# Mixer groups of a hybrid decoder layer: spreading a group's state product, scan and gate over later projection tiles

## The chip, the core and the metric

The kernel runs on one core of one Trainium2 chip. The metric is the device time of one execution in microseconds; the time before is the median of 3 runs. Six engines matter: TensorE (PE in the profile, with its weight loads as PEld), VectorE (DVE), ScalarE (ACT), GpSimd (POOL), and SyncE (SP), which issues most DMAs. Each engine takes its own instructions strictly in order; semaphores order them against the others.

## What is computed

One inference step of one decoder layer, for 256 prompt tokens and 8 sample tokens (one new token for each of 8 sequences), 264 columns in all. The model's width is 2048.

```python
h += 0.5 * RMSNorm(SwiGLU_1(RMSNorm(h)))
u = RMSNorm(h)
proj = u @ w_in            # GLU a, b: 2 x 1024; z: 3072; xBC: 5120; dt: 48
...
v = silu(layernorm(causal_dwconv(glu_a * sigmoid(glu_b), w=31)))
xbc = silu(causal_dwconv(xbc, w=4))
y, h_new = ssd(x, dt, a, B, C, d_skip, h0)
yg = y * silu(z)
yg = yg * rsqrt(mean(yg * yg, per group of 384 channels) + EPS) * norm_gain
h += RMSNorm(concat(v, yg) @ w_out)
h += 0.5 * RMSNorm(SwiGLU_2(RMSNorm(h)))
h += RMSNorm(sigmoid(RMSNorm(h) @ W_gate) * (p @ W_proj))
```

The state-space part (`ssd`) has 8 groups, each with its own B and C (128 states) and 6 heads of 64 channels (384 channels, 3 tiles of 128). For the prompt it runs in two chunks of 128 tokens. For the samples it needs C times the incoming state, summed over the 128 states: y = exp(a·dt)·(C·h0) + (B·C)·x·dt + d_skip·x.

## The kernel before

All activations lie transposed: channels on the 128 partitions, the 264 tokens along the free axis. A projection's output tile is 128 channels by 264 tokens and is summed in one accumulator (`acc`, PSUM, 5 buffers). For accuracy each weight is split in two: a DMA on SP's queue brings it (`wraw`), ScalarE's cast makes the high part (`whi`, L152), VectorE subtracts it for the low part (`wlo`, L153), and each block of 128x128 takes three matmuls (L247 to L249: `whi` with both parts of the activation, then `wlo` with the first). These steps go by half-tiles of 8 blocks; an output tile of the in-projection has two half-tiles, 48 matmuls. `wraw`, `whi` and `wlo` have four buffers each, and loads are issued two units ahead.

The layer runs as a first feed-forward (to about 793 us), the mixer's in-projection (817 to 1344), its out-projection with LayerNorm and residual (to 1586), the second feed-forward (to 2318), and a per-layer embedding. The change lies in the mixer.

The in-projection has 81 output tiles in the order `IN_ORDER` (L44): dt, then for each of 8 groups B, C, three x tiles (x0, x1, x2), three z tiles (z0, z1, z2). Pairs of tiles of the GLU (gb, ga), 8 of them, stand inside the groups that `GLU_IN` (L40) lists, behind x0, and the rest at the end. After each output tile the loop at L809 emits its own work: `do_conv` (L609) for B, C and x, a short convolution of three steps on VectorE and a Silu on ScalarE; `act(..., Silu)` for z; `do_glu` for ga, whose 30 taps of the long convolution (L216, `y<-v,vec,y`) go into a list `bg`; and then up to 4 pieces of `bg` (10 in the out-projection). When the last pair is done, `do_ln`, the LayerNorm over the GLU's channels, is put at the list's end; its results are read by the last eighth-parts of the out-projection (`gemm_pair(range(CM))`).

Three functions carry a group's own work:

- `ssd` (L697), emitted after x2. Its first part is the prompt's: transposes of x and B (L707, L708), B·C (L721), the chunk states (L733), the outputs (L748). Its second part is the samples': B and C of the samples as rows (L761, L762), through DRAM to all partitions (`cbc`), then six times: load a piece of the state (`h0`, 3 buffers; the profile calls it `h<-in_hst`), multiply it with `cbc` on GpSimd (L773), reduce it on VectorE (L774, `ych<-h`). Then the sample's y.
- `gate` (L789), emitted after x0 of the next group by `finish_gate`: y times silu(z) on VectorE (`h<-h,h 128x792`), three squares on ScalarE, two additions on GpSimd (`run<-run,tmp`), their sum over partitions by a matmul with ones (L299, in `SumSq.total`), logarithm and exponential, and the scaled output.
- `decays` (L676), after x0: the decay factors of a group.

What sets the order: the program is written once for all engines, and a scheduler places each engine's instructions by its own simulated times; what was written earlier has precedence among what is ready. Small matmuls take one of three PSUM buffers (`ps`) in turn. ScalarE's function tables are loaded by `table` (L231): Silu on one side, logarithm and exponential on the other need a load at each change, and the calls are kept in program order.

## Time and profile before

| what | value |
|---|---|
| median of 3 runs | 2449.36 us (2447.6 to 2455.64) |
| the profiled execution's own time | 2442.84 us |
| its span, first to last instruction | 2441.1 us |
| mean granted TensorE clock | 0.991 |

| stage, us from the span's start | TensorE idle, us | VectorE busy | ScalarE busy |
|---|---|---|---|
| in-projection, 817 to 1344 | 20.8 | 82% | 58% |
| out-projection with residual, 1344 to 1586 | 9.1 | 77% | 54% |
| second feed-forward, 1586 to 2318 | 2.9 | 57% | 42% |

A row of a timeline reads: start, duration in us, engine, line, operation, output <- inputs, how many in a row, and in brackets how long the engine stood idle before it and what ended that. A row of the waits: what waited <- what it waited for, then total us, times, longest. A row of the windows: the stretch and its length, busy time of each engine with instructions in brackets, the granted clock, the share of the DMA engines, GB/s. A row of the groups: count | busy us in total, mean ns of one | idle time before, and what ended it. Lines are those of the kernel before.

### The profile page before, as it was taken

The page shows a single profiled execution, that of the slowest core. Times are in us where ns is not written, and L with a number is a line of the kernel's source. Part 1 is how long each engine was busy: PE and PEld are TensorE (multiplying, and loading weights), DVE is VectorE, ACT ScalarE, POOL GpSimd, SP SyncE. Part 2 cuts the span into 40 slices and gives each one's busy share as a digit, 9 for nine tenths or more (in the row PEclk, how much of TensorE's full clock was granted, in tenths as well). Part 3 has the DMA queues.
Part 4 walks back from the last instruction along what each step waited for, and adds up shares of the span by engine and source line. Part 5 has one row for each costly group of instructions (what it writes and reads, how often), then busy time and mean ns, then how long its engine had stood idle before and what let it go on. Part 6 is the DMA issues. An engine that isn't in the chain of part 4 may idle for free.

```text
span 2441.1 us, 47358 instructions
## 1 busy us (share of the span) xinstructions
PE 2365.9 (97%) x19432; PEld 2339.6 (96%) x19432; DVE 1584.4 (65%) x2273; ACT 1179.6 (48%) x1761; POOL 357.2 (15%) x353
## 2 busy tenths in 40 slices
PE   8999999999999999999999999899999999999996
PEld 8999999999999889999999999899999999999996
DVE  6554455545557858989798975866545655555585
ACT  6444444433456465565655554644444443344463
POOL 2500000000015212121212111400000000000152
PEclk9999999999999999999999999999999999999998
DMA  7655555555556666676666557467666776675653
GB/s 246 216 183 184 183 183 184 185 184 182 182 172 213 197 202 197 202 223 204 206 214 199 180 168 234 139 234 244 231 207 228 243 235 207 222 237 194 196 172 115
DMA packets 165242, 489.89 MB, mean 201 GB/s; under 512 B 25456, under 2 KB 42272, under 8 KB 165024
## 3 DMA queue, kind: packets, MB, share of 16 engines
q1 hardware_dynamic: 165024, 486.86, 61.2%
q8 instruction: 152, 2.49, 0.4%
q14 instruction: 66, 0.54, 0.1%
HBM read 465.65 MB, written 22.42 MB: 200 GB/s over the span
## 4 chain that ended last, share of the span: by engine, by line
PE 82%; DVE 7%; DMA 4%; issue 3%; ACT 3%; POOL 1%; SPq 0%; ACTq 0%; DVEq 0%; POOLq 0%
PE acc L248 27%; PE acc L247 27%; PE acc L249 27%; DVE wlo L153 2%; ACT whi L152 1%; DMA h<-in_hst 1%; POOL h L213 1%; DVE h L213 1%; DVE y L216 1%; DVE tmp L216 1%; DVE act L216 1%; DMA cbc<-d_bc 1%; DMA wraw<-in_w 1%; PE ps L299 1%; POOL run L213 0%
## 5 line engine op out<-in xcount | busy, mean ns | idle before, releaser
L249 PE MATMUL acc<-act,wlo 128*128 128x264 f32 x6320 | 1796.9, 285 | 4.5 <-DVE wlo L153 4.4
L248 PE MATMUL acc<-act,whi 128*128 128x264 f32 x6320 | 1783.5, 283 | 14.6 <-DVE act L216 7.7
L247 PE MATMUL acc<-act,whi 128*128 128x264 f32 x6320 | 1766.0, 283 | 15.9 <-ACT whi L152 8.5
L153 DVE TENSOR_TENSOR wlo<-wraw,whi 128x1024 fp32r<-128x1024 f32 (+1 forms) x806 | 993.4, 1234 | 594.5 <-ACT whi L152 588.8
L152 ACT CAST whi<-wraw 128x1024 fp32r<-128x1024 f32 (+1 forms) x806 | 828.4, 1032 | 959.6 <-PE acc L248 710.9
L247 PEld LDWEIGHTS acc<-act,whi 128*128 128x128 f32 x6320 | 1190.5, 190 | 19.1 <-ACT whi L152 8.7
L248 PEld LDWEIGHTS acc<-act,whi 128*128 128x128 f32 x6320 | 1188.4, 188 | 20.3 <-DVE act L216 10.0
L249 PEld LDWEIGHTS acc<-act,wlo 128*128 128x128 f32 x6320 | 1187.2, 188 | 8.5 <-DVE wlo L153 6.7
L213 POOL TENSOR_TENSOR run<-run,tmp 128x264 f32<-128x264 f32 x135 | 129.7, 961 | 956.8 <-ACT tmp L240 953.3
L213 POOL TENSOR_TENSOR s<-s,eap 128x1024 f32<-128x1024 f32 x24 | 48.3, 2012 | 596.8 <-DMA s<-in_hst 573.2
L216 DVE SCALAR_TENSOR_TENSOR y<-v,vec,y 128x251 f32<-128x251 f32 (+23 forms) x240 | 117.2, 508 | 1.2
L213 POOL TENSOR_TENSOR h<-h,cbc 128x512 f32<-128x512 f32 x48 | 72.1, 1521 | 165.5 <-DMA cbc<-d_bc 77.8
L216 DVE SCALAR_TENSOR_TENSOR s<-bb,xds,s 128x128 f32<-128x128 f32 x192 | 52.6, 346 | 58.7 <-POOL s L213 58.7
L213 DVE TENSOR_TENSOR tmp<-acc,rr 128x264 f32<-128x264 f32 x104 | 44.8, 431 | 59.4 <-PE acc L249 59.2
L255 ACT CAST act<-tmp 128x264 fp32r<-128x264 f32 x120 | 48.7, 410 | 60.8 <-DVE tmp L213 47.1
L213 DVE TENSOR_TENSOR tmp<-tmp,acc 128x264 f32<-128x264 f32 x88 | 37.6, 428 | 41.0 <-PE acc L249 40.1
L213 DVE TENSOR_TENSOR act<-tmp,act 128x264 fp32r<-128x264 f32 x120 | 54.2, 457 | 0.0
L240 ACT ACTIVATE tmp<-tmp 128x264 f32<-128x264 f32 x112 | 47.0, 420 | 8.1 <-DVE tmp L213 7.8
L213 DVE TENSOR_TENSOR y<-y,acc 128x264 f32<-128x264 f32 x80 | 33.9, 424 | 23.9 <-PE acc L249 23.9
L240 ACT ACTIVATE tmp<-y 128x264 f32<-128x264 f32 x67 | 28.0, 425 | 43.6 <-DVE y L213 42.5
L774 DVE TENSOR_REDUCE ych<-h 128x4 f32<-128x512 f32 x48 | 32.4, 677 | 16.3 <-POOL h L213 16.2
L216 DVE SCALAR_TENSOR_TENSOR act<-h,vec,act 128x264 fp32r<-128x264 f32 x48 | 35.2, 755 | 6.5 <-ACT act L240 6.5
(148 smaller groups left out, 793.0 us busy)
## 6 DMA issues: line engine op xcount, KB each, us to landing
wraw<-in_w SPq DMA_DIRECT2D x774, 512.0 KB, 4.5
h<-in_hst SPq DMA_DIRECT2D x48, 256.0 KB, 4.1
s<-in_hst SPq DMA_DIRECT2D x24, 512.0 KB, 6.3
out_nss<-s SPq DMA_DIRECT2D x24, 512.0 KB, 2.8
wraw<-in_w SPq DMA_DIRECT2D x32, 256.0 KB, 3.8
ab<-d_cs SPq DMA_DIRECT2D x16, 384.0 KB, 4.8
cbc<-d_bc SPq DMA_DIRECT2D x8, 512.0 KB, 4.3
bb<-d_bc SPq DMA_DIRECT2D x8, 512.0 KB, 6.0
```

The costliest lines, as they stand in the source:

```text
L152: nc.scalar.copy(hi, raw)
L153: nc.vector.tensor_tensor(out=lo, in0=raw, in1=hi.bitcast(F32), op=ALU.subtract)
L213: return (eng or nc.vector).tensor_tensor(out=out, in0=in0, in1=in1, op=op)
L216: return nc.vector.scalar_tensor_tensor(out=out, in0=in0, scalar=scalar, in1=in1, op0=op0, op1=op1)
L240: i = nc.scalar.activation(out=out, in_=in_, func=func, bias=bias, scale=scale)
L247: nc.tensor.matmul(acc, hi, x[:, 0, :], start=first, stop=False)
L248: nc.tensor.matmul(acc, hi, x[:, 1, :], start=False, stop=False)
L249: nc.tensor.matmul(acc, lo, x[:, 0, :], start=False, stop=last)
L255: nc.scalar.copy(t[:, 0, :], x)
L299: nc.tensor.matmul(p, ones, s, start=i == 0, stop=i == len(self.parts) - 1)
L774: nc.vector.tensor_reduce(out=ych[:, j, b : b + 4], in_=h0, op=ALU.add, axis=AX.X)
```

## The change

A group's work is spread over later tiles. `ssd` keeps the prompt's part and is emitted after z0 instead of x2. The sample's part becomes three functions: `sample_rows` (the rows of B and C and their trip through DRAM) after x0; `sample_state` (two state pieces: load, product) after x1, x2 and z0, whose reductions are emitted at the next call, the last at z1; `sample_out` (the rest) after z2. `gate` becomes `gate_begin` (multiplication, squares, additions), emitted after the convolution of the next group's B, and `gate_end` (the sum, logarithm, exponential, output), after that of the next C. `GLU_IN` has three groups in place of four, so three pairs stand inside groups and five at the end. Which buffers `v` takes and when the mixer's memory is closed follow the length of `GLU_IN`, as before.

```diff
--- before.py
+++ after.py
@@ -37,7 +37,7 @@
 FF_CHUNKS = [(0, 16), (16, 32), (32, 44)]
 
 
-GLU_IN = (1, 2, 4, 6)
+GLU_IN = (1, 3, 5)
 
 
 
@@ -755,8 +755,10 @@
             nc.tensor.matmul(po[:, j, :], s0[:, P * j : P * j + P], cf[:, P:NP_], start=True, stop=True)
         tt(ea, ea, po, ALU.mult)
         tt(y[:, :, P:NP_], y[:, :, P:NP_], ea, ALU.add)
-
-        js = slice(3 * g, 3 * g + 3)
+        return y
+
+    def sample_rows(g, bf, cf):
+
         pr = ps_tile([P, 2, P])
         nc.tensor.transpose(pr[:NS, 0, :], bf[:, NP_:], ident)
         nc.tensor.transpose(pr[:NS, 1, :], cf[:, NP_:], ident)
@@ -766,12 +768,26 @@
         cbc = mp.tile([P, NS, P], F32, tag="cbc", bufs=1, name=nm("cbc"))
         nc.sync.dma_start(cbc, d_bc[g, 1].partition_broadcast(P))
         ych = mp.tile([P, 3, NS], F32, tag="ych", bufs=1, name=nm("ych"))
-        for j in range(3):
-            for b in range(0, NS, 4):
-                h0 = mp.tile([P, 4, P], F32, tag="h0", bufs=3, name=nm("h0"))
-                nc.sync.dma_start(h0, a["hst"][3 * g + j][:, b : b + 4, :])
-                tt(h0, h0, cbc[:, b : b + 4, :], ALU.mult, nc.gpsimd)
-                nc.vector.tensor_reduce(out=ych[:, j, b : b + 4], in_=h0, op=ALU.add, axis=AX.X)
+        return cbc, ych
+
+    products = []
+
+    def sample_state(g, j, cbc, ych):
+
+        while products:
+            o, h0 = products.pop(0)
+            nc.vector.tensor_reduce(out=o, in_=h0, op=ALU.add, axis=AX.X)
+        if j == 3:
+            return
+        for b in range(0, NS, 4):
+            h0 = mp.tile([P, 4, P], F32, tag="h0", bufs=3, name=nm("h0"))
+            nc.sync.dma_start(h0, a["hst"][3 * g + j][:, b : b + 4, :])
+            tt(h0, h0, cbc[:, b : b + 4, :], ALU.mult, nc.gpsimd)
+            products.append((ych[:, j, b : b + 4], h0))
+
+    def sample_out(g, bf, cf, xt, ych, y):
+
+        js = slice(3 * g, 3 * g + 3)
         prod = mp.tile([P, NS], F32, tag="prod", bufs=1, name=nm("prod"))
         tt(prod, bf[:, NP_:], cf[:, NP_:], ALU.mult)
         pcs = ps_tile([P, NS])
@@ -784,13 +800,16 @@
         o = _COLS["dsk"][0] + 3 * g
         tt(sy, xt[:, :, NP_:], vec[:, o : o + 3].unsqueeze(2).to_broadcast([P, 3, NS]), ALU.mult)
         tt(y[:, :, NP_:], ych, sy, ALU.add)
-        return y
-
-    def gate(g, y, zs):
+
+    def gate_begin(g, y, zs):
+
         tt(y, y, zs, ALU.mult)
         sq = SumSq(3, direct=0)
         for j in range(3):
             sq.add(y[:, j, :])
+        return g, y, sq
+
+    def gate_end(g, y, sq):
         t = tmp()
         rsqrt(t, sq.total(), eps1, 1.0 / 384)
         for j in range(3):
@@ -799,12 +818,16 @@
             stt(o, y[:, j, :], V("sng", 3 * g + j), t, ALU.mult, ALU.mult)
             keep(k, o)
 
+    def begin_gate():
+        if gated:
+            summed.append(gate_begin(*gated.pop()))
+
     def finish_gate():
-        if pend:
-            gate(*pend.pop())
+        if summed:
+            gate_end(*summed.pop())
 
     first = gemm_first(us, k16, 4)
-    pend = []
+    gated, summed = [], []
     nglu = 0
     for n, (kind, m) in enumerate(IN_ORDER):
         acc = first[n] if n < 4 else gemm_one(us, k16)
@@ -813,27 +836,36 @@
         elif kind == "B":
             bct = mp.tile([P, 2, T], F32, tag="bc", bufs=2, name=nm("bc"))
             do_conv(acc, m - MT_X, bct[:, 0, :])
+            begin_gate()
         elif kind == "C":
             do_conv(acc, m - MT_X, bct[:, 1, :])
+            finish_gate()
         elif kind == "x":
             g, j = divmod(m - MT_X, 3)
             if j == 0:
                 xt = h_tile()[:, :3, :]
             do_conv(acc, m - MT_X, xt[:, j, :])
             if j == 0:
-                finish_gate()
                 ab, ea = decays(g)
-            if j == 2:
-                y = ssd(g, bct[:, 0, :], bct[:, 1, :], xt, ab, ea)
+                cbc, ych = sample_rows(g, bct[:, 0, :], bct[:, 1, :])
+            else:
+                sample_state(g, j - 1, cbc, ych)
         elif kind == "z":
             g, j = divmod(m - MT_Z, 3)
             if j == 0:
                 zs = h_tile()[:, :3, :]
             act(zs[:, j, :], acc, AF.Silu)
-            if j == 2:
-                pend.append((g, y, zs))
+            if j == 0:
+                y = ssd(g, bct[:, 0, :], bct[:, 1, :], xt, ab, ea)
+            if j < 2:
+                sample_state(g, j + 2, cbc, ych)
+            else:
+                sample_out(g, bct[:, 0, :], bct[:, 1, :], xt, ych, y)
+                gated.append((g, y, zs))
         elif kind == "gb":
             pb = acc
+            if nglu == len(GLU_IN):
+                begin_gate()
         elif kind == "ga":
             do_glu(nglu, pb, acc)
             nglu += 1
```

What this does to the instructions of an engine in its own order, at three places. A row has the line, the operation, the output and its inputs with their numbers, and the shape.

VectorE at the gate of group 2, before: `h_598<-h_598,h_632 128x792` is the gate's multiplication, `wlo175_0` the low part of the half-tile's weights during which TensorE takes the sum of this gate.

```order
L216 SCALAR_TENSOR_TENSOR h_639_12006<-acc_655_12135,vec_75,h_639_12006 128x253
L216 SCALAR_TENSOR_TENSOR y_595_11341<-v_594_11335,vec_75,y_595_11341 128x226
L213 TENSOR_TENSOR h_598_11489<-ych_621_11563,sy_630_11594 128x3x8
L153 TENSOR_TENSOR wlo175_0_12382<-wraw175_0_12380,whi175_0_12381 128x1024
L213 TENSOR_TENSOR h_598_11489<-h_598_11489,h_632_11664 128x792
L153 TENSOR_TENSOR wlo175_8_12388<-wraw175_8_12386,whi175_8_12387 128x1024
L153 TENSOR_TENSOR wlo176_0_12444<-wraw176_0_12442,whi176_0_12443 128x1024
L153 TENSOR_TENSOR wlo176_8_12450<-wraw176_8_12448,whi176_8_12449 128x1024
L216 SCALAR_TENSOR_TENSOR tmp_645_12029<-h_598_11489,vec_75,tmp_643_12023 128x264
```

After: the multiplication is `h_604<-h_604,h_603`, and the half-tile in question is `wlo169_0`.

```order
L216 SCALAR_TENSOR_TENSOR bc_632_11712<-acc_636_11729,vec_75,bc_632_11712 128x253
L213 TENSOR_TENSOR ych_595_11225<-ych_595_11225,sy_630_11646 128x24
L213 TENSOR_TENSOR sy_630_11646<-h_588_11185,vec_75 128x24
L213 TENSOR_TENSOR h_604_11440<-ych_595_11225,sy_630_11646 128x3x8
L213 TENSOR_TENSOR h_604_11440<-h_604_11440,h_603_11438 128x792
L153 TENSOR_TENSOR wlo169_0_11821<-wraw169_0_11819,whi169_0_11820 128x1024
L213 TENSOR_TENSOR prod_690_12488<-bc_632_11712 128x8
L153 TENSOR_TENSOR wlo169_8_11827<-wraw169_8_11825,whi169_8_11826 128x1024
L216 SCALAR_TENSOR_TENSOR h_646_11879<-acc_645_11818,vec_75,h_646_11879 128x255
```

The split of that half-tile stood one row ahead of the multiplication and now stands directly behind it.

TensorE at the same gate, before: the sum is the L299 row.

```order
L247 MATMUL acc_692_12441<-act_454_9304,whi174_8_12324 128x264
L248 MATMUL acc_692_12441<-act_454_9304,whi174_8_12324 128x264
L249 MATMUL acc_692_12441<-act_454_9304,wlo174_8_12325 128x264
L247 MATMUL acc_693_12503<-act_411_9190,whi175_0_12381 128x264
L299 MATMUL ps_644_12024<-run_640_12015,ones_81 128x264
L707 MATMUL ps_657_12207<-ident_76,h_639_12006 128x128
L707 MATMUL ps_660_12216<-ident_76,h_639_12006 128x128
```

And after:

```order
L249 MATMUL acc_655_11981<-act_426_9230,wlo169_0_11821 128x264
L247 MATMUL acc_655_11981<-act_429_9238,whi169_0_11820 128x264
L248 MATMUL acc_655_11981<-act_429_9238,whi169_0_11820 128x264
L299 MATMUL ps_638_11798<-run_633_11721,ones_81 128x264
L763 MATMUL ps_650_11911<-ident_76,bc_632_11712 8x128
L764 MATMUL ps_650_11911<-ident_76,bc_632_11712 8x128
L249 MATMUL acc_655_11981<-act_429_9238,wlo169_0_11821 128x264
```

The sum stood behind the first matmul of its half-tile (`whi175_0`); it now stands behind the twentieth of its half-tile (`whi169_0`), with two sample transposes behind it (L763, L764 are the former L761, L762). The sum of the other gates stands behind 2, 11, 5, 2, 5, 14 and 3 matmuls of its half-tile before (gates 0, 1, 3 to 7), and behind 16, 14, 19, 13, 18, 19 and 4 after; the split of that half-tile stands ahead of the multiplication at all eight before, and behind it at gates 1, 2, 4 and 6 after.

TensorE in group 0, before: the second set of transposes for the prompt's part (L707, L708), between two tiles.

```order
L249 MATMUL acc_512_10167<-act_454_9304,wlo148_8_10045 128x264
L707 MATMUL ps_474_9802<-ident_76,h_467_9633 128x128
L707 MATMUL ps_477_9811<-ident_76,h_467_9633 128x128
L707 MATMUL ps_474_9802<-ident_76,h_467_9633 128x128
L708 MATMUL ps_474_9802<-ident_76,bc_465_9616 128x128
L707 MATMUL ps_477_9811<-ident_76,h_467_9633 128x128
L708 MATMUL ps_477_9811<-ident_76,bc_465_9616 128x128
L247 MATMUL acc_513_10235<-act_411_9190,whi149_0_10100 128x264
```

And after:

```order
L249 MATMUL acc_524_10265<-act_426_9230,wlo149_0_10101 128x264
L247 MATMUL acc_524_10265<-act_429_9238,whi149_0_10100 128x264
L248 MATMUL acc_524_10265<-act_429_9238,whi149_0_10100 128x264
L707 MATMUL ps_484_9888<-ident_76,h_467_9633 128x128
L707 MATMUL ps_487_9897<-ident_76,h_467_9633 128x128
L707 MATMUL ps_484_9888<-ident_76,h_467_9633 128x128
L708 MATMUL ps_484_9888<-ident_76,bc_465_9616 128x128
L707 MATMUL ps_487_9897<-ident_76,h_467_9633 128x128
L708 MATMUL ps_487_9897<-ident_76,bc_465_9616 128x128
L249 MATMUL acc_524_10265<-act_429_9238,wlo149_0_10101 128x264
```

The same six transposes stood between the last matmul of a tile and the first of the next; they now stand twenty matmuls into the next tile (`whi149_0` is the same half-tile in both).

ScalarE's order has 41 table loads in the whole program instead of 27; the small matmuls of the mixer stand in 68 places between the projection's instead of 74.

## The prediction

> **What bounds the kernel now.** I read the page first: busy time by engine, then the windows by stage, then TensorE's waits inside the mixer, then the timeline at its two longest kinds of wait.

> ```profile
> PE 2365.9 (97%) x19432; PEld 2339.6 (96%) x19432; DVE 1584.4 (65%) x2273; ACT 1179.6 (48%) x1761; POOL 357.2 (15%) x353
> ...
> core 0: us, PE busy (x) PEld busy (x) DVE busy (x) ACT busy (x) POOL busy (x), PEclk, DMA share, GB/s
> 122.00:671.00 549.00, 549.00 (x4578) 549.00 (x4577) 278.60 (x302) 224.22 (x270) 0.00 (x0) 1.00 0.57 183
> 817.00:1344.00 527.00, 506.20 (x4120) 489.25 (x4120) 432.28 (x737) 304.86 (x555) 95.96 (x72) 0.99 0.65 204
> 1344.00:1464.00 120.00, 119.59 (x988) 119.10 (x989) 102.23 (x182) 64.42 (x99) 16.28 (x14) 1.00 0.54 175
> ```

> TensorE is busy 97% of the span, so the matmul stream sets the end. The first window shows what it does undisturbed: 4578 matmuls in 549 us, 0.12 us each. The second is the mixer's in-projection, the only stage that the change rewrites: of 527 us TensorE stands idle in 20.8 (527.00 − 506.20). No engine beside it is full: VectorE has 94.7 us idle there, ScalarE 222. The third window is the first part of the out-projection, with 0.4 us idle. So what the change can win is about 21 us of stalls with what follows them, and no more.

> ```profile
> PE ps L299 <- POOL run L213: 10.6, 8, 2.5
> PE ps L707 <- ACT h L240: 6.1, 2, 4.5
> PE acc L249 <- DVE wlo L153: 3.1, 6, 0.7
> PE ps L733 <- ACT btm L716: 1.1, 1, 1.1
> ```

> These four rows (total, times, longest, in us) are all of it, 20.9 us. The eight waits at L299 are the eight gates: the sum of squares is a matmul with ones, and TensorE, which takes its work in order, reaches it before GpSimd has added the squares. All eight:

> ```profile
> 917.04 0.97 DVE L213 TENSOR_TENSOR h<-h,h 128x792 f32<-128x792 f32 x1
> 918.33 1.21 DVE L153 TENSOR_TENSOR wlo<-wraw,whi 128x1024 fp32r<-128x1024 f32 x1
> 918.38 0.72 ACT L240 ACTIVATE tmp<-h 128x264 f32<-128x264 f32 x2
> 918.86 3.02 POOL L213 TENSOR_TENSOR run<-run,tmp 128x264 f32<-128x264 f32 x2 [6.23 <-ACT tmp L240]
> 921.94 0.71 PE L299 MATMUL ps<-run,ones 128*128 128x264 f32 x2 [2.47 <-POOL run L213]
> ...
> 985.24 0.71 PE L299 MATMUL ps<-run,ones 128*128 128x264 f32 x2 [1.36 <-POOL run L213]
> ...
> 1053.72 0.71 PE L299 MATMUL ps<-run,ones 128*128 128x264 f32 x2 [0.81 <-POOL run L213]
> ...
> 1099.74 0.98 DVE L213 TENSOR_TENSOR h<-h,h 128x792 f32<-128x792 f32 x1
> 1100.64 1.22 DVE L153 TENSOR_TENSOR wlo<-wraw,whi 128x1024 fp32r<-128x1024 f32 x1
> 1101.63 1.67 POOL L213 TENSOR_TENSOR run<-run,tmp 128x264 f32<-128x264 f32 x2 [4.54 <-ACT tmp L240]
> 1103.35 0.71 PE L299 MATMUL ps<-run,ones 128*128 128x264 f32 x2 [0.60 <-POOL run L213]
> ...
> 1168.39 3.04 POOL L213 TENSOR_TENSOR run<-run,tmp 128x264 f32<-128x264 f32 x2 [13.05 <-ACT tmp L240]
> 1171.48 1.00 PE L299 MATMUL ps<-run,ones 128*128 128x264 f32 x2 [2.20 <-POOL run L213]
> ...
> 1290.97 0.71 PE L299 MATMUL ps<-run,ones 128*128 128x264 f32 x2 [0.89 <-POOL run L213]
> ```

> Two gates are shown whole. Counting gates from 0, gate 0: the multiplication ends at 918.01, TensorE arrives at 919.47 (921.94 − 2.47), 1.46 us later, and the sum can start 3.93 us after the multiplication. Gate 3: it ends at 1100.72, TensorE arrives 2.03 us later, the sum starts 2.63 us after it. The two differ by GpSimd's pair of additions, 3.02 us against 1.67. So a gate's wait is the chain after the multiplication (2.63 to 3.93) less TensorE's arrival (1.5 to 2.0). Gates 5 and 7, not shown, have the remaining 2.3 of the 10.6.

> A long stall costs more than itself:

> ```profile
> 922.60:926.00 3.40, 3.40 (x18) 3.40 (x17) 1.67 (x4) 3.28 (x8) 0.00 (x0) 0.50 0.79 234
> 926.00:929.40 3.40, 3.40 (x30) 3.40 (x30) 1.60 (x4) 2.75 (x7) 0.00 (x0) 1.00 0.29 108
> 985.30:988.70 3.40, 3.40 (x27) 3.29 (x28) 3.40 (x7) 3.13 (x6) 0.00 (x0) 1.00 0.65 199
> 1171.80:1175.20 3.40, 3.40 (x16) 3.15 (x15) 2.52 (x4) 2.90 (x6) 0.00 (x0) 0.50 0.73 206
> ```

> Behind the waits of 2.47 and 2.20 us the granted clock is 0.50 for one window and 18 matmuls run where 30 do afterwards: 12 × 0.12 = 1.4 us lost. Behind the wait of 1.36 us the clock stays at 1.00. The point lies between 1.36 and 2.20 us here.

> [...]

> **The change part by part.**

> *Gates.* The multiplication and the squares are now issued after the next B tile and the sum after the next C tile. Written two tiles (11.5 us at 0.12 × 48 a tile) apart, all 10.6 us would go. But the scheduler places by its own readiness, and the orders say less. The sum still stands a few matmuls into a half-tile, a short way behind the multiplication. What changes: at gates 1, 2, 4 and 6 the weight split for that same half-tile now stands behind the multiplication on VectorE, where before it stood ahead at all eight. So TensorE can't get to the sum before the split has ended and the products in front of the sum have run. At gate 2 that is 1.22 for the split and 18 products of 0.12 (20 stand ahead of the sum, the first two use the other half of the weight and need no split): 3.4 us. In the same way 3.1, 2.5 and 3.3 us at gates 1 (a tap of some 0.5 lies between), 4 and 6. With the long chain, 3.93, their waits become 0.8, 0.5, 1.4 and 0.6, 3.3 in place of 5.3 (1.36 + 0.81 + 2.20 + 0.89): 2.0 saved. With the short one, 2.63, 0.1 is left: 5.2 saved. The split directly behind the multiplication runs beside GpSimd's additions as at gate 0, whose pair was the long one, so I take **−2.3**, near the long end. Gates 0, 3, 5 and 7 stay. Gate 4 falls to about 1.4 us, no longer than the stall that kept its clock: **−1.4** (0 if it stays over the point).

> *The second stall of group 0.*

> ```profile
> 861.12 0.36 ACT L240 ACTIVATE eap<-eap 128x192 f32<-128x192 f32 x1 [7.29 <-DMA eap<-d_dt]
> ...
> 864.15 0.44 PE L707 MATMUL ps<-ident,h 128*128 128x128 f32 x2 [4.52 <-ACT h L240]
> ...
> 876.06 0.64 PE L707 MATMUL ps<-ident,h 128*128 128x128 f32 x3 [1.53 <-ACT h L240]
> ```

> Of the 6.1 us at L707 the first 4.52 come from a DMA that ScalarE waits for (7.29 us), which the change doesn't touch: it stays. The second, 1.53, belongs to the transposes that stood directly ahead of a tile; they now stand 20 matmuls into it, 2.4 us later. ScalarE gets one more copy in front of them, priced at the 0.36 of the small activation above: 2.4 > 1.9, **−1.5** (bounds −1.5 and 0, if a table load of 1.28 lands there too). The wait at L733 belongs to the same group; 59 matmuls stand between the transposes and it now, 48 before, 1.3 us more than its 1.1: **−1.1** (bounds −1.1 and 0).

> *State product and its reductions.*

> ```profile
> L774 DVE TENSOR_REDUCE ych<-h 128x4 f32<-128x512 f32 x48 | 32.4, 677 | 16.3 <-POOL h L213 16.2
> ...
> L213 POOL TENSOR_TENSOR h<-h,cbc 128x512 f32<-128x512 f32 x48 | 72.1, 1521 | 165.5 <-DMA cbc<-d_bc 77.8 <-DVE wlo L153 35.5 <-DMA h<-in_hst 24.4
> ```

> The same 48 products and reductions with their DMAs are issued, six a group, but two at x1, two at x2 and two at z0, each pair's reductions a tile later, instead of six in a row. VectorE stood 16.2 us behind GpSimd there, and splits queued behind a waiting reduction: that is what I make of the six waits for a split, 3.1 us. A reduction issued a tile (5.7 us) after its product (1.5 us) seldom waits. But SP's queue now gets state loads between weight loads at three tiles instead of one, and two of the three buffers are held a tile longer, so a load can wait for its buffer and the weights behind it on SP with it. Bounds −3.1 and +5: if the weights came late at two of a group's three loading tiles, 16 waits at the mean of the six (3.1 / 6 = 0.5 us) make 8 in place of 3.1. I take **−2.0**, nearer the row. The prompt's state-space part moves from x2 to z0 with every matmul it had, and its successor, the gate, moves too.

> *Small matmuls.* They stand in 68 clusters between the products instead of 74. A cluster costs a gap of about 0.1 us, one product's time: **−0.7** (0 to −0.7).

> *Table loads.*

> ```profile
> L235 ACT ACT_TABLE_LOAD x18 | 23.1, 1283 | 0.3
> ```

> The sequence on ScalarE gets 14 more, since Silu at z alternates with the gate's logarithm and exponential and with decays at more places: 14 × 1.283 = 18.0 us. ScalarE has 222 us idle in the stage and the weight casts run up to 10 us ahead: **0**. If each stood before something that TensorE waits for, +18.

> *GLU pair.* One pair less among the groups, so 30 taps leave the mixer for the out-projection:

> ```profile
> L216 DVE SCALAR_TENSOR_TENSOR y<-v,vec,y 128x239 f32<-128x239 f32 (+28 forms) x104 | 45.1, 478 | 0.2
> ...
> 1465.57 0.77 DVE L213 TENSOR_TENSOR act<-y,act 128x264 fp32r<-128x264 f32 x2
> ...
> 1495.76 0.43 DVE L213 TENSOR_TENSOR y<-y,acc 128x264 f32<-128x264 f32 x1 [0.69 <-PE acc L249]
> ```

> 30 × 0.478 = 14.3 us. The LayerNorm behind the taps has its last output split at 1466; the tile that reads it hands its sum over at 1495.76, after 48 matmuls, so it starts at 1490. The cover is 24 us. VectorE is busy in 102 of that stage's 120 us, so the taps shift the LayerNorm's end by nearly all of their 14; some 10 us of cover are left: **0**. Without cover, +14.

> Sum: −2.3 − 1.4 − 1.5 − 1.1 − 2.0 − 0.7 = **−9.0 us**. The profiled execution took 2442.84 (span 2441.1), so 2433.8 on its scale; the median of the three runs is 2449.36, 6.5 above it. Carried to the median: **2440.4**.

> **The rivals.**

> *The waits stay where they are.* The sum of squares comes in the order at the same kind of place: 4 to 20 matmuls into a half-tile. If VectorE runs as far ahead of TensorE as before, the later split doesn't hold TensorE and the same waits are found at new places, 10.6 again; with the stalls of group 0 filled by the new table loads nothing is won. Time 2449. For it: four of eight gates have the old order. Against: four have not.

> *All waits of the mixer go but the first.* If VectorE's lead makes the multiplication early, the written distance of two tiles takes hold: 10.6 + 2 × 1.4 (both half clocks) + 1.5 + 3.1 + 1.1 + 0.7 = 19.8 us, so 2429.5. Against it: the order has the split for the very half-tile behind the multiplication, so the two are near each other in time.

> *Slower: GpSimd's additions run beside splits at every gate.* The two lengths of the pair, 3.02 and 1.67, go with what VectorE does beside it, and at gates 1, 2, 4 and 6 a split now follows the multiplication at once.

> ```profile
> L213 POOL TENSOR_TENSOR run<-run,tmp 128x264 f32<-128x264 f32 x16 | 16.3, 1016 | 72.0 <-ACT tmp L240 71.4
> ```

> The mean of 1.016 us an addition means most pairs are short now. With 3.0 us at all eight and TensorE as early as at gate 0, each waits 2.4 and pays 1.4 for the clock: 8 × 3.8 = 30.4 against 13.4 (10.6 + 2 × 1.4) now, +17.0; with the −5.3 of the other terms +11.7, **2461**. It decides when the wait passes the point between 1.36 and 2.20 at most gates; below it, it is worth a few us only. Against it: a later arrival goes with the very splits that lengthen the pair.

> [...]

> **How the numbers follow.** The forecast 0.48, with a range of its own of 2436 to 2445 (down by the bounds of gates and splits, −5.2 and −3.1 in place of −2.3 and −2.0; up by the splits at 0 and no half clock saved, 3.4, with half of group 0's 2.6). Waits stay: 0.22. All go: 0.14. Slower: 0.13. Others, a table load or a state load on the path among them: 0.03. From 2427 to 2453 holds the first three cases; the fourth is left out with the rest, 0.16 and some edge. The measurement of this kernel tells about 0.3%, 7.35 us, from no change: faster means below 2442.0. The forecast's range is about six tenths below that, "all go" nearly all: 0.29 + 0.13 + some 0.04 of the second = 0.46. Slower is the fourth with a little of the first two and of the rest, 0.16; no change the remaining 0.38.

> **What would show it.** Right: waits at L299 of 8 to 9 us in the mixer with the four later gates shorter; half clock at gate 0 and not at gate 4; the wait of 4.5 us at L707 still there and the second gone; the reductions' wait for GpSimd well below 16 us; 32 or so table loads and no wait of TensorE for what stands behind them. Wrong: L299 at 0, or at 15 and more with pairs of 3 us; waits for a split above 3 us, with loads of the state late on SP; TensorE waiting at the end of the out-projection for the LayerNorm.

## The result and the profile after

| | median | lowest to highest | runs |
|---|---|---|---|
| before | 2448.79 us | 2441.55 to 2455.64 | 13 |
| after | 2458.27 us | 2455.14 to 2466.2 | 13 |

The ratio on record is 1.0052 with a 95% interval of 1.004 to 1.0065: the change makes the kernel 0.5% slower. (The medians alone lie 9.5 us or 0.4% apart.) The profiled execution of after took 2456.28 us, its span is 2454.6, 13.5 more than before. What follows accounts for this one pair of profiles.

Which stage has it? The page's busy times of after, and the window over the mixer's in-projection, whose end lies 13.5 us later (columns as before):

```profile
PE 2371.8 (97%) x19432; PEld 2346.1 (96%) x19432; DVE 1578.8 (64%) x2273; ACT 1198.2 (49%) x1775; POOL 352.4 (14%) x353
...
817.00:1357.50 540.50, 510.43 (x4116) 493.92 (x4116) 430.45 (x739) 325.29 (x580) 95.92 (x74) 0.98 0.64 200
```

The same 19432 matmuls as before, and 30.1 us in which TensorE is idle where there were 20.8. From the first matmul of this stage on, the same 4425 matmuls take 577.8 us where they took 564.8; every other stretch of the program differs by 1 us or less. So nearly all 13 us lie here. TensorE's waits in it:

```profile
PE acc L249 <- DVE wlo L153: 23.3, 10, 5.2
PE ps L763 <- ACT bc L240: 3.7, 1, 3.7
PE acc L247 <- DVE bc L216: 1.4, 1, 1.4
PE ps L299 <- POOL run L213: 0.8, 1, 0.8
PE ps L733 <- DVE xde L213: 0.7, 2, 0.5
PE ps L707 <- ACT h L240: 0.2, 1, 0.2
```

The gates' 10.6 us at L299 are down to 0.8, one wait. In their place TensorE waits for weight splits, 23.3 us in ten waits where 3.1 us in six stood. The waits at L707 and L733 (7.2 before) are down to 0.9, but 5.1 have come under new names: in group 0 the row transposes (L763), which now come first, wait for the Silu of B, which stands behind the same DMA on ScalarE as the transposes of before did (`eap<-d_dt`; ScalarE stood 6.49 us there, before 7.29), and a tile waits for a convolution.

The stalls make 8.9 of the 13 us. Another 5.4 are clock. In stretches of granted clock 0.50 the products follow each other every 0.22 us instead of every 0.12. Before, the stage has three such stretches, at waits of 4.52, 2.47 and 2.20 us, and loses 4.3 us in them; after, it has six, at waits of 3.70, 2.50, 3.81, 5.23, 2.62 and 4.41 us, and loses 9.7. The rows show two of the six, at the waits of 2.62 and 4.41 us, and the window behind a wait of 1.57 us, which kept its clock (the granted clock is the third number from the end):

```profile
1110.00:1113.40 3.40, 3.06 (x14) 3.06 (x15) 3.40 (x6) 0.00 (x0) 3.40 (x2) 0.50 0.56 139
1171.40:1174.80 3.40, 3.40 (x17) 3.40 (x17) 3.40 (x3) 0.00 (x0) 0.94 (x1) 0.50 0.83 237
...
1294.40:1297.80 3.40, 3.19 (x25) 2.98 (x25) 3.40 (x6) 0.00 (x0) 2.30 (x2) 1.00 0.77 209
```

The gaps around the small matmuls are 1.6 us less than before, single slow distances at full clock 0.4 us more. 8.9 + 5.4 − 1.6 + 0.4 makes the 13.

What holds up a split? The longest wait, in group 3, by the timelines of VectorE, ScalarE, GpSimd, SP and TensorE:

```profile
1024.75 0.27 PE L763 MATMUL ps<-ident,bc 128*8 128x128 f32 x1
1026.11 0.35 ACT L766 COPY rows<-ps 8x256 f32<-8x256 f32 x1
1026.96 0.29 SPq L767 DMA_DIRECT2D d_bc<-rows  x1
1029.56 1.22 DVE L153 TENSOR_TENSOR wlo<-wraw,whi 128x1024 fp32r<-128x1024 f32 x1
1031.51 0.33 SPq L769 DMA_DIRECT2D cbc<-d_bc  x1
1036.11 3.95 POOL L213 TENSOR_TENSOR h<-h,cbc 128x512 f32<-128x512 f32 x3 [12.28 <-issue]
1037.45 0.69 DVE L779 TENSOR_REDUCE ych<-h 128x4 f32<-128x512 f32 x1 [6.67 <-POOL h L213]
1041.21 2.28 DVE L153 TENSOR_TENSOR wlo<-wraw,whi 128x1024 fp32r<-128x1024 f32 x1
1043.54 0.59 PE L249 MATMUL acc<-act,wlo 128*128 128x264 f32 x1 [5.23 <-DVE wlo L153]
```

The sample rows of B and C are transposed from 1024.75 on and written to DRAM at 1026.96; C's are read back, spread over the partitions, from 1031.51; the first product starts at 1036.11, 11.4 us after the transposes began. VectorE has reached the first reduction at 1030.8 and stands there 6.67 us. Queued behind it are a second reduction, three splits of a gate's output, and the next weight split, which takes 2.28 us here where the one ahead of the wait took 1.22. TensorE uses up the splits that it had and waits 5.23 us. Before, in the same group, VectorE came later to the reduction:

```profile
1075.71 0.27 PE L762 MATMUL ps<-ident,bc 128*8 128x128 f32 x1
...
1086.56 0.69 DVE L774 TENSOR_REDUCE ych<-h 128x4 f32<-128x512 f32 x1 [0.79 <-POOL h L213]
```

It arrives 10.1 us after the transposes and waits 0.79. Read in this way for groups 1 to 7, VectorE reaches the first reduction 10.4 us after the row transposes before and 7.4 after (means), and the reduction starts at 11.3 and 11.5: the trip is nearly the same, the place in VectorE's order isn't. The orders say it too, with 0.12 us for each of the projection's products: the split behind a group's first reduction is needed by TensorE 15 to 17 us after the row transposes before (groups 1 to 7), and 10 to 13 after. In group 3 that is 17 and 12, and 11.4 for the trip with a product, a reduction and a split behind it don't fit into 12.

### The profile page after: what moved, and what is told of

It reads as the page before. It is cut to its first block, busy times and chain, and to the rows that moved or that the text cites. A ratio compares the mean times of both kernels' runs of the same rounds, so it can differ in the third digit from the quotient of the medians.

```text
span 2454.6 us, 47385 instructions
## 1 busy us (share of the span) xinstructions
PE 2371.8 (97%) x19432; PEld 2346.1 (96%) x19432; DVE 1578.8 (64%) x2273; ACT 1198.2 (49%) x1775; POOL 352.4 (14%) x353
## 4 chain that ended last, share of the span: by engine, by line
PE 82%; DVE 7%; DMA 4%; ACT 4%; issue 3%; POOL 1%; SPq 0%; ACTq 0%; DVEq 0%; POOLq 0%
PE acc L249 27%; PE acc L247 27%; PE acc L248 27%; DVE wlo L153 2%; DMA ab<-d_cs 1%; ACT whi L152 1%; DMA cbc<-d_bc 1%; ACT ab L240 1%; DVE tmp L216 1%; DVE act L213 1%; DMA d_bc<-rows 1%; DVE h L213 1%; DMA wraw<-in_w 1%; DVE ych L779 0%; ACT tmp L240 0%
## 5 line engine op out<-in xcount | busy, mean ns | idle before, releaser
L249 PE MATMUL acc<-act,wlo 128*128 128x264 f32 x6320 | 1799.7, 286 | 24.6 <-DVE wlo L153 24.3
L248 PE MATMUL acc<-act,whi 128*128 128x264 f32 x6320 | 1785.9, 283 | 13.5 <-DVE act L216 6.8
L153 DVE TENSOR_TENSOR wlo<-wraw,whi 128x1024 fp32r<-128x1024 f32 (+1 forms) x806 | 995.2, 1236 | 608.4 <-ACT whi L152 602.3
L249 PEld LDWEIGHTS acc<-act,wlo 128*128 128x128 f32 x6320 | 1189.7, 189 | 29.5 <-DVE wlo L153 28.0
L247 PEld LDWEIGHTS acc<-act,whi 128*128 128x128 f32 x6320 | 1193.6, 190 | 20.7 <-ACT whi L152 8.5
L213 POOL TENSOR_TENSOR run<-run,tmp 128x264 f32<-128x264 f32 x135 | 126.9, 940 | 1020.2 <-ACT tmp L240 1017.7
L213 POOL TENSOR_TENSOR s<-s,eap 128x1024 f32<-128x1024 f32 x24 | 46.5, 1936 | 597.3 <-DMA s<-in_hst 556.8
L216 DVE SCALAR_TENSOR_TENSOR y<-v,vec,y 128x255 f32<-128x255 f32 (+23 forms) x240 | 109.4, 487 | 0.6
L216 DVE SCALAR_TENSOR_TENSOR s<-bb,xds,s 128x128 f32<-128x128 f32 x192 | 52.6, 348 | 68.4 <-POOL s L213 68.4
L213 POOL TENSOR_TENSOR h<-h,cbc 128x512 f32<-128x512 f32 x48 | 70.4, 1486 | 174.5 <-DMA cbc<-d_bc 127.8
L213 DVE TENSOR_TENSOR tmp<-acc,rr 128x264 f32<-128x264 f32 x104 | 44.8, 431 | 55.7 <-PE acc L249 55.6
L213 DVE TENSOR_TENSOR tmp<-tmp,acc 128x264 f32<-128x264 f32 x88 | 37.7, 429 | 41.4 <-PE acc L249 40.2
L213 DVE TENSOR_TENSOR act<-tmp,act 128x264 fp32r<-128x264 f32 x120 | 62.0, 524 | 0.0
L235 ACT ACT_TABLE_LOAD x41 | 52.6, 1283 | 1.5 <-PEq L1095 0.8
L240 ACT ACTIVATE tmp<-tmp 128x264 f32<-128x264 f32 x112 | 47.2, 422 | 9.4 <-DVE tmp L213 9.3
L213 DVE TENSOR_TENSOR y<-y,acc 128x264 f32<-128x264 f32 x80 | 34.0, 425 | 24.2 <-PE acc L249 24.2
L240 ACT ACTIVATE tmp<-y 128x264 f32<-128x264 f32 x67 | 28.1, 426 | 43.6 <-DVE y L213 42.5
```

What stands on the lines that cost most here:

```text
L153: nc.vector.tensor_tensor(out=lo, in0=raw, in1=hi.bitcast(F32), op=ALU.subtract)
L213: return (eng or nc.vector).tensor_tensor(out=out, in0=in0, in1=in1, op=op)
L216: return nc.vector.scalar_tensor_tensor(out=out, in0=in0, scalar=scalar, in1=in1, op0=op0, op1=op1)
L235: after(nc.scalar.preload_act_table_set(name).ins)
L240: i = nc.scalar.activation(out=out, in_=in_, func=func, bias=bias, scale=scale)
L247: nc.tensor.matmul(acc, hi, x[:, 0, :], start=first, stop=False)
```

## The experiments

Two theories were put against each other at first. *Trip* (later called *reductions*): the above. *Tables*: the 14 further table loads delay casts and so splits. All ratios are to the kernel before, measured alongside; the columns on the right are from one profile each, over the same 4425 matmuls, in us; half clock is the time that products lost in stretches of granted clock 0.50.

| kernel | ratio, 95% interval | gates | splits | all stalls | half clock |
|---|---|---|---|---|---|
| before | 1 | 10.6 | 3.1 | 21.2 | 4.3 |
| after | 1.0052, 1.0040 to 1.0065 | 0.8 | 23.3 | 30.1 | 9.7 |
| rows_at_c | 1.0057, 1.0037 to 1.0077 | 0.0 | 26.2 | 31.6 | 12.4 |
| state_later | 1.0056, 1.0038 to 1.0074 | 1.1 | 22.8 | 29.5 | 11.6 |
| cbc_input | 1.0056, 1.0039 to 1.0073 | 0.8 | 23.3 | 29.5 | 10.4 |
| held | 1.0032, 1.0019 to 1.0045 | 6.7 | 7.2 | 25.9 | 3.1 |
| held_mm | 1.0014, 1.0002 to 1.0025 | 2.0 | 16.0 | 23.2 | 5.3 |
| gate_alone_2 | 1.0102, 1.0083 to 1.0122 | 15.6 | 1.5 | 37.5 | 10.7 |
| glu_alone | 1.0045, 1.0031 to 1.0060 | 16.2 | 0.9 | 26.0 | 7.7 |
| state_alone | 1.0025, 1.0012 to 1.0039 | 2.0 | 6.4 | 29.8 | 5.4 |
| gate_back | 1.0042, 1.0027 to 1.0056 | 1.1 | 10.4 | 28.5 | 3.3 |
| glu_back | 1.0063, 1.0050 to 1.0076 | 0.0 | 23.2 | 33.9 | 11.1 |
| scan_back | 1.0097, 1.0084 to 1.0110 | 1.5 | 20.7 | 36.6 | 10.7 |
| tables | 1.0022, 1.0009 to 1.0035 | 11.8 | 0.9 | 24.7 | 5.0 |
| held_state_alone | 1.0006, 0.9994 to 1.0018 | 3.9 | 1.0 | 22.0 | 3.0 |
| held_mm_state | 1.0025, 1.0015 to 1.0035 | 4.3 | 6.0 | 27.2 | 6.5 |
| sum_held | 1.0026, 1.0015 to 1.0036 | 12.9 | 4.3 | 22.4 | 7.4 |

**Begin the trip earlier, or the product later.** Both are edits of where the code is written.

```diff
         elif kind == "C":
             do_conv(acc, m - MT_X, bct[:, 1, :])
             finish_gate()
+            cbc, ych = sample_rows(m - MT_CM, bct[:, 0, :], bct[:, 1, :])
...
-                cbc, ych = sample_rows(g, bct[:, 0, :], bct[:, 1, :])
```

> The changed kernel with sample_rows emitted after the convolution of C instead of x0, one output tile (5.7 us) earlier. Theory 'trip': in the changed kernel a group's first reductions stand on VectorE before cbc has come back from its trip through DRAM, the weight splits queue behind them, and TensorE waits (23.3 us for wlo, against 3.1 before). With the trip begun 5.7 us earlier that falls to 6 us or less, VectorE's wait for GpSimd at the reductions from 31 us to under 12, and the ratio to the kernel before is 0.992 to 0.997, since the gates' waits (10.6 before, 0.8 after) stay away. Theory 'tables': 14 more table loads on ScalarE delay casts and so splits; there are still 41, so the ratio stays 1.004 to 1.006.

```diff
-            else:
-                sample_state(g, j - 1, cbc, ych)
+            elif j == 2:
+                sample_state(g, 0, cbc, ych)
...
-            if j < 2:
-                sample_state(g, j + 2, cbc, ych)
-            else:
+            sample_state(g, j + 1, cbc, ych)
+            if j == 2:
```

> The changed kernel with the state's products one tile later (x2, z0, z1) and the reductions with them (z0, z1, z2). Theory 'trip': the first reductions have 5.7 us more for cbc to come back; waits for wlo 6 us or less, ratio 0.992 to 0.998. Theory 'tables': 41 loads as in the changed kernel, ratio 1.004 to 1.006.

Neither came in: 1.0057 and 1.0056, and the waits are those of after. Both ratios are what *tables* had set, 1.004 to 1.006. But neither run tested the theory. In both, every engine's instructions and DMA issues stand in exactly the order of after: moving these lines in the program by a tile moved nothing. So the two are repeats of after, and they show how far one profile's columns vary by themselves: splits 22.8 to 26.2 us, half clock 9.7 to 12.4. That later code is later execution is the first thing that the forecast had wrong too.

**Shorten the trip.** The load of `cbc` takes an input instead, behind the row write in the order (`behind`, shown below) but without waiting for it to land. So this kernel leaves out the samples' C in their state product.

```diff
...
-        nc.sync.dma_start(cbc, d_bc[g, 1].partition_broadcast(P))
+        rd = nc.sync.dma_start(cbc, a["hst"][3 * g])
+        behind(rd.ins, wr.ins)
```

> The changed kernel with one load changed: cbc is filled from an input tensor of the same 512 KB, right behind the write of the rows and without waiting for it to land (leaves out the samples' C in their state product; the row write and every other instruction stay). In the traces the write takes about 4.5 us to land and the load behind it about 4.8. Theory 'trip': the reductions stay 10 to 14 us behind the row transposes by the order, and the trip shrinks from some 12.5 to some 8 us, so they no longer wait long: waits for wlo from 23 us to 6 or less, ratio 0.994 to 0.999. Theory 'tables' (the 14 further table loads delay casts and splits): they are still there, ratio 1.004 to 1.006.

A miss: 1.0056, the ratio of *tables* again. The first reductions start 9.8 us after the transposes (mean of groups 1 to 7) instead of 11.5, but the order has changed too: VectorE waits 4.4 us a group for the first reduction, in after 4.1, and the splits' waits are 23.3 us in both. In groups 3 and 5, where the order has the split at the same distance as in after, the first reduction starts 3.3 and 2.2 us sooner and the longest split waits are 3.4 us each; after and its two repeats have 3.9 to 6.2 and 4.4 to 5.8. In group 2 the split waits rise from 4.2 to 6.5. So the sum doesn't decide between the theories, and the two comparable groups speak, weakly, for the trip.

**Hold the reductions.** The first real test, since the place in VectorE's order is set by hand:

```diff
+    def behind(ins, first):
+        tc.add_manual_dep(ins, first.name, ...)
...
-            nc.vector.tensor_reduce(out=o, in_=h0, op=ALU.add, axis=AX.X)
+            r = nc.vector.tensor_reduce(out=o, in_=h0, op=ALU.add, axis=AX.X)
+            behind(r.ins, order["last"])
```

> The changed kernel with every reduction held, in VectorE's order, behind the last activation of the tile after whose work it is emitted: in groups 1 to 7 the split behind a group's first reduction is needed 24 to 30 us after the row transposes, in place of 10 to 13. Theory 'trip': waits for wlo 6 us or less; the sample's output and the gate come later, so up to 10 us of the gates' waits may come back; ratio 0.994 to 1.002. Theory 'tables': 41 loads, waits for wlo of 15 us or more, ratio 1.004 to 1.006.

The splits' waits fall from 23.3 to 7.2 (one of 4.2 us is left), half clock from 9.7 to 3.1, and 0.2% of the time with them. The gates wait 6.7 us again, as was feared. 7.2 is a little over the bound that was set, 1.0032 a little over the ratio.

In held_mm the hold is the last matmul of the tile instead of the last activation (`order["mm"]`), and by the order it takes effect in groups 3 and 5 alone. So one kernel holds both cases.

> The changed kernel with every reduction held in VectorE's order behind the last matmul of the tile after whose work it is emitted. By the order this moves the reductions of groups 3 and 5 alone (the split behind the first one is needed 21 and 25 us after the row transposes, 12 and 13 in the changed kernel); the other groups stay. Theory 'reductions': the waits for wlo of 5.2 us in group 3 and 4.4 us in group 5 (by the profile of the changed kernel) go below 1 us each, those of the other groups stay within 1 us or so of what they were: in sum 23.3 to some 13, ratio 1.001 to 1.004. Theory 'tables': all groups stay as they are.

VectorE in group 3 of held_mm (row transposes at 1026.8):

```profile
1031.87 1.22 DVE L153 TENSOR_TENSOR wlo<-wraw,whi 128x1024 fp32r<-128x1024 f32 x1
1037.24 5.69 DVE L153 TENSOR_TENSOR wlo<-wraw,whi 128x1024 fp32r<-128x1024 f32 x3 [0.45 <-ACT whi L152]
1044.58 1.26 DVE L786 TENSOR_REDUCE ych<-h 128x4 f32<-128x512 f32 x2
```

Three splits now stand ahead of the reductions, which find their products done. The waits of 5.2 us in group 3 and 4.4 in group 5 are gone, with one of 1.2 left later in group 3; those of the other groups remain (3.5, 3.3, 2.7 and 2.7 the longest in groups 1, 2, 4 and 6, where after has 2.5, 3.8, 2.6 and 1.5). The sum is 16.0 where some 13 was expected. TensorE's waits in held_mm:

```profile
PE acc L256 <- DVE wlo L153: 16.0, 9, 3.5
PE ps L770 <- ACT bc L247: 3.4, 1, 3.4
PE ps L306 <- POOL run L213: 2.0, 3, 1.1
```

With 41 table loads as in after, the ratio is 1.0014. This settles the splits: the long waits go where the reductions are moved, and elsewhere they stay within some 1.2 us. As the cause of these waits *tables* is out; what the loads cost elsewhere is another question.

**One part alone.** Three kernels have one part of the change in the kernel before.

```diff
+            begin_gate()     # after do_conv of B
...
+            finish_gate()    # after do_conv of C
...
-                finish_gate()    # after do_conv of x0
```

> The kernel before with one part of the change alone: the gate's first half after the next B, its sum after the next C. Theory 'trip': the reductions are where they were, so the waits for wlo stay near 3 us, the gates' 10.6 us go to 2 or less with most of the half-clock stretches behind them: ratio 0.993 to 0.997, with the 41 table loads of the changed kernel. Theory 'tables': the loads come with this part, so it is the part that makes the kernel slower: ratio 1.003 or more and waits for wlo of 10 us or more.

> The kernel before with the gate's split alone once more, for a profile that can be read. It came out at 1.0093. Theory 'trip' has no answer to that: by the order the split behind a group's first reduction is needed 13 to 18 us after the row transposes, as before (15 to 17), so waits for wlo stay below 8 us and something else must show, 30 us of it. Theory 'tables': waits on ScalarE's results (casts, convolutions, transposes) of 15 us or more in sum.

The gate's split alone is the worst of the parts: 1.0093, interval 1.0073 to 1.0114, and 1.0102 in the second measurement, which has the profile. Splits wait for 1.5 us only, so the theory of the reductions holds there, but its main expectation failed: the gates' waits rise from 10.6 to 15.6 in place of 2. Another 8.0 us are waits for `btm`, a copy on ScalarE, where before has 1.1; TensorE's waits for ScalarE are 14.3 us in all, just under the 15 that *tables* had set.

```profile
PE ps L299 <- POOL run L213: 14.0, 7, 4.4
PE ps L733 <- ACT btm L716: 8.0, 2, 4.2
PE ps L707 <- ACT h L240: 4.8, 2, 4.0
```

(These rows of gate_alone_2 end at 1360 us, ahead of its last gate.) The longest wait for `btm`, at 1066.8, has three table loads on ScalarE ahead of it, and ScalarE runs on without a pause from the first of them to the copy:

```profile
1054.72 1.28 ACT L235 ACT_TABLE_LOAD   x1
1056.46 1.28 ACT L235 ACT_TABLE_LOAD   x1
1059.75 1.28 ACT L235 ACT_TABLE_LOAD   x1
...
1066.50 0.27 ACT L716 COPY btm<-ps 128x128 f32<-128x128 f32 x1
```

In the kernel before, one load stands at this place, ScalarE pauses 0.79 us ahead of the copy, and TensorE doesn't wait for it. The other of the two waits looks the same. So in this kernel the loads lie on the path of these waits, with two more than before, 2.6 us of the 4.2, and *tables* has its part here. Why the gates wait longer is open.

```diff
-GLU_IN = (1, 2, 4, 6)
+GLU_IN = (1, 3, 5)
```

> The kernel before with the other GLU_IN alone: three pairs inside the groups, five behind. By the order the reductions stand as before (15 to 17 us). Both theories: nothing is lost here and the 14 us of taps stay under the tail's cover; ratio 0.998 to 1.002. If the pair were the cause: 1.004 or more, with TensorE waiting at the out-projection's end.

A miss for both theories: 1.0045, with no wait at the out-projection's end beyond those of before. The gates wait 16.2 us instead of 10.6, though nothing about a gate was edited. By the profile three of its pairs of additions take 3.0 us, where before has two.

The third has the gate and `GLU_IN` of before in the changed kernel, so the moved state product and scan are left; its edit is the two others' undone.

> The changed kernel with the gate after x0 and GLU_IN (1, 2, 4, 6) as before: the state product and the prompt's scan moved, nothing else; 27 table loads. Theory 'reductions': VectorE stands at a group's first reduction 10 to 12 us after the row transposes in the kernel before and 5 to 11 us in the changed one, while the products need 10 to 12.6 us in every run, so VectorE waits there and the splits behind it are late. This part alone then has waits for wlo of 8 us or more (10.4 with the gate back and the other GLU_IN) and gate waits of 3 us or less, as there; ratio 1.001 to 1.005. Theory 'tables': ratio 0.998 to 1.001, waits for wlo below 5 us.

The ratio, 1.0025, and the gates, 2.0 us, are as expected. Splits have 6.4, a little under the 8 that was set; 15.1 us are waits for Silu of x at the transposes (L707), which the theory didn't name. Held_state_alone, below, has 1.5 of them; that they come from VectorE's waits at the reductions is likely and not shown.

**One part taken back.** The gate as before (gate_back), the other pairs (glu_back), the scan at x2 again (scan_back), each in the changed kernel.

> The changed kernel with the whole gate after x0 again, as before; 27 table loads as before. Theory 'trip': the waits for wlo stay at 15 us or more and the gates' waits come back in part (5 to 11 us): ratio 1.006 to 1.012. Theory 'tables': with the loads gone the waits for wlo go to 6 us or less; ratio 0.999 to 1.002.

1.0042, between the two expectations. With 27 table loads the splits still wait 10.4 us, so the loads aren't needed for it; whether they had a share in the 12.9 us that went can't be told here, since the order changed too and 10.7 us now stand at the transposes (L707). And the gates, unsplit and after x0 as before, wait 1.1 us: so the gate's split isn't what frees them.

> The changed kernel with GLU_IN (1, 2, 4, 6) as before. The other GLU_IN alone cost 1.0045 in the kernel before, where the forecast had 0. If its 30 taps or the pair's place cost that by themselves, this kernel gets it back: ratio 0.999 to 1.002 in place of 1.0052. If the cost was that of the shifted order in the kernel before (gate waits 10.6 to 16.2 there), which the changed kernel hasn't since its gates wait for nothing, it stays at 1.003 to 1.007, with the waits for wlo where the order puts a first reduction 10 to 13 us behind the row transposes (groups 1 to 5) and little in group 7 (18 us).

1.0063, the second case: nothing is got back.

> The changed kernel with the prompt's state-space part after x2 again; the sample pipeline, the gate's split and GLU_IN stay as changed. Theory 'reductions': the multiplication comes long after the last reduction (9 to 36 us in the changed kernel) since the state product begins at x1; so the gate waits stay at 3 us or less without the scan's move, and the reductions still stand ahead of the trip (10 to 14 us by the order): waits for wlo 12 us or more; ratio 1.002 to 1.007. If the scan's move were what frees the gates: gate waits 8 us or more.

The gates wait 1.5 us, so they are freed without the scan's move; with gate_alone and glu_alone, where they aren't, this leaves the state product. The ratio, 1.0097, is above what was expected; one stall of 5.9 us behind VectorE in group 0 is part of it. Of the parts taken back, the scan's place at z0 is the one that clearly helps the others: without it the kernel is 0.45% slower than after.

**The table loads by themselves.** In the kernel before, `table(LN_EXP)` after each C.

> The kernel before with the logarithm's table loaded behind every group's C, where nothing needs it: 10 more table loads (37 in place of 27), 12.8 us of ScalarE, nothing else added; the order shifts a little with them. Theory 'reductions': ScalarE has over 200 us idle in the stage, the loads themselves cost 0 to 3 us; ratio 0.999 to 1.003 with what the order's shift does. Theory 'tables': 1.28 us of path for most of them, ratio 1.004 or more, with TensorE waiting for ScalarE's results (casts, btm, transposes of h) 8 us longer than before.

1.0022, inside the first range, but not free. The profile has 43 table loads, 16 more than before and not the 10 that were expected. TensorE's waits for ScalarE don't grow, 6.7 us against 7.2. The order shifts with the loads (one new wait of 3.8 us stands at a convolution in group 0), so the loads' own price can't be told from the shift's.

**Towards a faster kernel.** Holding the reductions in state_alone, by activation and by matmul:

> state_alone with every reduction held, in VectorE's order, behind the last activation of the tile after whose work it is emitted. Theory 'reductions': waits for wlo go from 8 us or more to 5 or less and VectorE's wait at the reductions below 12 us; if the gate waits stay small the kernel beats the one before, ratio 0.995 to 0.999; if they come back with the later sample output (6.7 us in the held kernel), 0.999 to 1.002. Theory 'tables': no effect, ratio as state_alone.

> state_alone with every reduction held in VectorE's order behind the last matmul of the tile after whose work it is emitted. By the order this moves groups 2, 4, 6 and 7 (20 to 25 us behind the row transposes, before 14 to 15). Theory 'reductions': in those groups the waits for wlo and those behind a late VectorE go, in groups 1, 3 and 5 they stay: waits for wlo 6.4 to 4 or less; ratio 0.998 to 1.002 against 1.0025 of state_alone.

Fully held, splits wait 1.0 us and the ratio is 1.0006, no different from before: 8.8 us have moved to a matmul of the scan that waits for VectorE (`xde`, the matmul of L733 before). Held by matmul, in half the groups, it stays at 1.0025: splits wait 6.0 in place of 4 or less, all of it in groups 3 and 5, which weren't moved, and the gates 4.3.

In the kernel before, the sum of squares held back by itself:

```diff
-            do_conv(acc, m - MT_X, xt[:, j, :])
-            if j == 0:
+            if j == 1:
                 finish_gate()
+            do_conv(acc, m - MT_X, xt[:, j, :])
+            if j == 0:
                 ab, ea = decays(g)
...
+                if held:
+                    behind(r.ins, order["mm"])
```

> The kernel before with the gate emitted a tile later (x1, ahead of its convolution) and its sum's matmul held, in TensorE's order, behind the eighth block of that tile; nothing else moves, 27 table loads, the reductions stand as before. By the order the sum then stands some 3.5 us later against the multiplication at gates 2 to 6, and as before at 0, 1 and 7. Theory 'reductions': the gate waits before are the same late reductions seen from the other side (multiplication 2 to 8 us behind the last reduction, sum 1.5 to 2.0 us behind the multiplication), so a later sum alone wins them without a wait for splits: gate waits 10.6 to some 5.5, waits for wlo 3 us or so, one half-clock stretch fewer; 6 us, ratio 0.996 to 0.999. Rival: the later sum delays the output and with it VectorE, and other waits take its place: 0.999 to 1.003.

A miss, 1.0026: TensorE does come to the sum 2.5 to 3.8 us after the multiplication at gates 2 to 6, where it came 1.7 to 2.0 after. But the squares and additions, written later too, end later as well: the sum can start 3.4 to 5.2 us behind the multiplication, before 2.6 to 4.0. The gates wait 12.9. No kernel tried here beats the one before.

## Why the prediction was wrong, by its steps

It forecast 2440.4 us, faster, and the kernel is slower; 2458.27 lies outside the range. By the terms of its sum:

- **The step that failed: splits and reductions, −2.0, measured +20.2** (3.1 to 23.3), and with half clock more. It said: "A reduction issued a tile (5.7 us) after its product (1.5 us) seldom waits." Two things are wrong in it. The product's 1.5 us is not what the reduction waits for, but the trip of C's rows through DRAM ahead of it, 9.1 to 12.6 us from transposes to first reduction in groups 1 to 7 of before and after. And a tile later in the program isn't a tile later in VectorE's order: in state_later, with the code a tile later still, the order is that of after to the last instruction. The rows for it were at hand. It quoted GpSimd as idle for `cbc` ahead of the products, 77.8 us, and took the 16.2 us that VectorE stood at the reductions as something that the change would remove. What it didn't ask is how far behind the row transposes the reductions stand in the new order, 10 to 13 us in place of 15 to 17, against a trip whose length GpSimd's wait for `cbc` shows. The 16.2 us didn't go, they nearly doubled:

```profile
L779 DVE TENSOR_REDUCE ych<-h 128x4 f32<-128x512 f32 x48 | 32.5, 676 | 31.0 <-POOL h L213 31.0
```

- **Gates, −2.3, measured −9.8.** The forecast took the gates' arrival from the order as a lower bound and used it as the value: 2.5 to 3.4 us after the multiplication. In after TensorE comes 4.1 to 9.0 us after it. At gate 2, for instance:

```profile
1014.29 0.98 DVE L213 TENSOR_TENSOR h<-h,h 128x792 f32<-128x792 f32 x1
1022.24 1.59 POOL L213 TENSOR_TENSOR run<-run,tmp 128x264 f32<-128x264 f32 x2 [17.20 <-ACT tmp L240]
1024.30 0.61 PE L299 MATMUL ps<-run,ones 128*128 128x264 f32 x2
```

  The multiplication ends at 1015.27, the sum comes 9.0 us later and waits for nothing. Before, the multiplication stood 2 to 8 us behind the last reduction of its group; in after, 10 to 36 us. gate_back, scan_back and gate_alone together show that it is this, the early state product, and neither the gate's split nor the scan, that does it; no run has the state product moved by itself. So the rival "all waits of the mixer go" was right about the gates and missed what replaces them.
- **Half clock, −1.4, measured +5.4.** The gates' two stretches are gone, as their stalls are; the splits' longer waits bring five in their place. The forecast's point between 1.36 and 2.20 us, above which a wait costs clock, isn't there: in held_mm a wait of 2.67 us left the clock at 1.00, in sum_held one of 1.31, with 0.28 shortly ahead of it, brought 0.50. In these traces it goes by how much idle time falls into one step of the clock, 3.41 us long (last section): 1.9 us of idle in one was enough in all 71 cases. So whether a wait of this length costs clock is in part luck.
- **Group 0, −1.5 and −1.1, measured −1.2** (7.2 to 6.0 with the new ones). Both waits nearly went, as forecast. The 4.5 us that were to stay at L707 became 3.7 at the row transposes, and 1.4 behind a convolution are new.
- **Small matmuls, −0.7**: the gaps are 1.6 us less. **Table loads, 0**: 32 in the stage as counted, and TensorE's waits for ScalarE are 3.9 us, before 7.2. But 0 doesn't hold for every place: in gate_alone_2 the loads lie on the path of two waits, 8.0 us, and sixteen loads in the kernel before came with 0.2%.
- **GLU pair, 0.** The cover at the out-projection's end held: its waits are those of before. Alone, though, the other `GLU_IN` costs 0.45%, mostly at the gates; inside the change, glu_back shows no cost.
- **The rival on the slower side** had the right sign and the wrong cause. It had longer additions on GpSimd; they are shorter:

```profile
L213 POOL TENSOR_TENSOR run<-run,tmp 128x264 f32<-128x264 f32 x16 | 13.8, 864 | 137.9 <-ACT tmp L240 137.3
```

  A mean of 864 ns instead of 1016, and no gate waits for them but one.

What stays open: why the gate's split alone and the other `GLU_IN` alone make the gates wait longer in the kernel before. In both the multiplication still follows the last reduction by 2 to 9 us, and TensorE comes 2.4 us behind the multiplication's end at the latest, at some gates earlier than before (in gate_alone_2 once 1.8 us ahead of it). That is how it looks, not why the scheduler chooses so.

## What to carry to other kernels

When work moves from one place in an in-order queue to another, ask how much time the old place left to the slowest of its inputs: a long latency may have fitted there by chance, and the move uncovers it for everything queued behind (here 23.3 us of waits for splits in place of 3.1). Where a scheduler places by simulated times, later code isn't later execution (rows_at_c, state_later). That it reckons with a shorter trip than the real one fits these runs and isn't shown, as its times aren't on record. A consumer that stands too early can be held by an explicit dependency (held, held_mm), but that may delay the next consumer (the gates waited 6.7 us in held, 0.8 in after). The parts' effects don't add: alone they cost 1.0, 0.45 and 0.25%, together 0.5%.
